# Hybrid mixer of a two-layer model: decay rows through DRAM, a side-by-side dt product, folded squares and a new order

## The chip, the cores and the metric

The kernel runs on one core of a Trainium2 chip, as one program and one launch. The metric is the device time of one execution in microseconds (us); lower is better. Three executions of the kernel before took 1096.77, 1097.22 and 1097.34 us, so the median is 1097.22 us. Durations below come from one further execution under the profiler.

The engines are named as in the profile: PE is the matrix engine (PEld its weight loads), DVE the vector engine, ACT the scalar engine, POOL is GpSimd, SP only issues transfers here. Each engine works through its own list of instructions in order. A tile is at most 128 partitions wide; "128x256" is 128 partitions by 256 elements.

## The reference

The model has two layers on 256 tokens of width 1024, all in float32. Layer 0 is FFN, hybrid mixer, FFN; layer 1 is FFN, mLSTM, FFN. A modulated RMS norm stands ahead of each. The change lies in the hybrid mixer alone:

```python
def hybrid_mixer(h, ...):
    gate_lru, x_lru, z_ssd, xbc, dt_raw = jnp.split(h @ w_in, HYB_SPLITS, axis=-1)
    x_lru = causal_conv(x_lru, lru_conv_w, lru_conv_b)
    y_lru = rg_lru(x_lru, ...) * jax.nn.gelu(gate_lru)
    xbc = jax.nn.silu(causal_conv(xbc, ssd_conv_w, ssd_conv_b))
    xs, bm, cm = ...                                   # 16 heads of 64, 2 groups, state 128
    dt = jax.nn.softplus(dt_raw + ssd_dt_bias)
    y = ssd_chunked(xs, dt, -jnp.exp(ssd_a_log), bm, cm) + ssd_d[:, None] * xs
    y = y * jax.nn.silu(z_ssd)
    y = rms_norm(y, in 2 groups of 512)
    return concatenate([y_lru, y]) @ w_out

def ssd_chunked(x, dt, a, bm, cm):                     # 2 chunks of 128 tokens
    acs = jnp.cumsum(dt * a, axis=-1)                  # per head and chunk
    decay_in = exp(acs[l] - acs[s]) for s <= l, else 0
    y_diag = einsum(cb * decay_in, x * dt)             # cb = C B^T of the chunk
    y_off = einsum(C, state of the chunk before) * exp(acs)
```

## The kernel before

Everything is held transposed: features on partitions, 256 tokens along the row. All weights come as one stream of 366 **pieces** of 512 KB (8 tiles of 128x128), sent by SP into four `wraw` buffers. ACT rounds each piece to `whi` (line 101), DVE takes the rest `wlo` (line 102); these two are the **weight split** of a piece. There are six pairs of buffers for split pieces. A weight product is three matmuls, `whi` by the high and the low part of the activation and `wlo` by the high part (lines 443, 444 and 445; `project`).

A scheduler in the framework sets the order of the instructions on each engine when the program is built, by priority and dependence. The kernel steers it in a few places. `stand(ins, s, n)` puts a PE instruction right behind the n-th weight product of stage s, `SUMS` holds such places for the sums of squares. `in_one_go` keeps a group of PE instructions together. `W.behind(i, n, ins)` orders the split n (0 is ACT's, 1 is DVE's) of piece i behind an instruction. `ADA_PLAN` spreads 144 blocks of the modulation (a 512 KB transfer and one 128x1024 DVE instruction each, line 262) over the pieces of the stages; 8 of them are in the hybrid stage, at its pieces 22 to 37.

The hybrid stage runs from about 199 to 375 us of the span. In order:

- `begin` computes B and C of the ssd; then come `xbc` 0 to 7, each a product, an ACT pass and three DVE taps (line 733) of the convolution. Behind them stand the `dtT` product (lines 818 to 820, 8 row tiles by three matmuls with the 16 columns of dt), softplus as a series in small DVE steps, the running sums `acs`, and their transpose `acst`.
- Ten steps follow with `xl` (product, ACT, three taps), `z` and the gates of the recurrence `ri`, and with the ssd's values and states in between.
- Then four **pairs** m0 = 0, 2, 4, 6 of 128 features (4 heads each). The rows of `acs` must stand on all 128 partitions. So DVE puts a high and a low part of the rows into `stk` (lines 864 and 865), and four `ab` matmuls a pair (line 974) spread them through a selector `sel` into two PSUM banks. ACT makes eight Relus of 128x128 from them (line 983), two Exps for `ce` (line 985) and one Exp over `mt` (line 986). DVE multiplies `mt` by `cb` (line 988) and `ce` by C (line 992). The 24 products `y` follow on PE (line 1008), DVE takes them out (lines 1012 and 1014), ACT squares them (lines 1018 and 1021). Behind each pair stand two `gl` products, the gate of the recurrence.
- Behind pairs 2 and 6 the squares of a group are summed over partitions (`rst_g`, line 359: two halves by two token blocks, so four matmuls of a 128x1 result, which the profile shows as eight), a chain of nine small DVE steps takes the inverse root (lines 373 and 320 to 329), and `rsb_g` (line 405) spreads it.
- `od`, the output product, reads the ssd's features 0 to 3 (`ysb`), then 4 to 7, then those of the recurrence (`ylb`), which come out of scans (line 1057) and a multiplication (line 1066).

## Time and profile before

| | |
|---|---|
| median of three executions | 1097.22 us |
| the profiled execution | 1097.25 us |
| its span (first to last instruction) | 1095.5 us |
| around the span | 1.75 us |
| PE busy | 1083.8 us, 99% |
| DVE busy | 920.5 us, 84% |
| ACT busy | 639.5 us, 58% |
| granted PE clock | 0.999 |
| moved by the DMA | 272.34 MB |

Busy times are averages over stages with different limits. Matmuls overlap: a row's mean for one matmul is longer than the step from one start to the next, so a count of matmuls is turned into time by the step. A stage's own limit is seen where an engine is busy for its whole window, and in PE's gaps with the instruction that ended each.

### The profile page before, as it was taken

To read this page: it belongs to the slowest core of one execution; us is meant where nothing else is said; L and a number is where in the kernel's file an instruction comes from. 1 tells how busy PE (TensorE), PEld (TensorE's weight loads), DVE (VectorE), ACT (ScalarE), POOL (GpSimd) and SP (SyncE) were. 2 spreads that over 40 slices of the span, in tenths; PEclk is the share of its full clock that TensorE was granted. 3 is DMA by queue.
4 is the path that set the end of the run, shared out by engine and by line. 5 is a ranking of instruction groups with operands and counts; after the bars stand their busy time and mean duration, and the time that the engine had idled before them with its cause. 6 is when DMAs were issued, how large, how long until landed. Compare 5 with 4: busy or idle time off the path is not lost.

```text
span 1095.5 us, 23272 instructions
## 1 busy us (share of the span) xinstructions
PE 1083.8 (99%) x9315; PEld 1070.4 (98%) x9315; DVE 920.5 (84%) x1654; ACT 639.5 (58%) x1053; POOL 8.8 (1%) x28
## 2 busy tenths in 40 slices
PE   9999999999999999999999999999999999999997
PEld 7999999999999999999999999999999999999997
DVE  7999999899999899989698798979768868866552
ACT  5765555678986564554454455448776655544452
POOL 0000000000000000000000000010000000000000
PEclk9999999999999999999999999999999999999999
DMA  9889999556855489999848799963432664875551
GB/s 375 344 318 391 387 352 343 178 196 195 279 167 191 139 307 370 354 351 327 281 142 323 266 356 346 338 204 119 146 102 81 208 193 137 298 239 193 193 174 39
DMA packets 75534, 272.34 MB, mean 249 GB/s; under 512 B 8593, under 2 KB 9393, under 8 KB 75426
## 3 DMA queue, kind: packets, MB, share of 16 engines
q1 hardware_dynamic: 74592, 269.38, 69.7%
q8 instruction: 73, 1.20, 0.4%
q0 software_dynamic: 400, 1.04, 0.4%
q10 hardware_dynamic: 434, 0.43, 0.1%
q14 instruction: 35, 0.29, 0.1%
HBM read 269.77 MB, written 1.05 MB: 247 GB/s over the span
## 4 chain that ended last, share of the span: by engine, by line
PE 80%; DVE 12%; DMA 4%; issue 2%; ACT 1%; ACTq 0%; DVEq 0%; SPq 0%
PE gu L445 12%; PE gu L444 12%; PE gu L443 11%; PE od L445 10%; PE od L443 10%; PE od L444 10%; DVE wlo L102 4%; DMA wraw<-in_wst_dram 3%; PE zz L445 1%; PE zz L443 1%; PE zz L444 1%; DMA wgr<-in_ml_wg_dram 1%; DVE ada L262 1%; DVE xc L733 1%; PE gu_f L509 1%
## 5 line engine op out<-in xcount | busy, mean ns | idle before, releaser
L102 DVE TENSOR_TENSOR wlo<-wraw,whi 128x1024 fp32r<-128x1024 f32 x364 | 442.9, 1221 | 83.6 <-ACT whi L101 83.0
L101 ACT CAST whi<-wraw 128x1024 fp32r<-128x1024 f32 x364 | 378.2, 1050 | 210.9 <-DMA wraw<-in_wst_dram 80.2
L444 PE MATMUL gu<-hb,whi 128*128 128x256 f32 x1296 | 358.0, 276 | 0.4 <-DVE hb L668 0.3
L443 PE MATMUL gu<-hb,whi 128*128 128x256 f32 x1296 | 358.0, 276 | 0.0
L445 PE MATMUL gu<-hb,wlo 128*128 128x256 f32 x1296 | 357.9, 276 | 0.1
L444 PEld LDWEIGHTS gu<-hb,whi 128*128 128x128 f32 x1296 | 243.3, 188 | 0.8 <-DVE hb L668 0.8
L445 PEld LDWEIGHTS gu<-hb,wlo 128*128 128x128 f32 x1296 | 243.3, 188 | 0.2 <-DVE wlo L102 0.2
L443 PEld LDWEIGHTS gu<-hb,whi 128*128 128x128 f32 x1296 | 243.2, 188 | 0.0
L443 PE MATMUL od<-ph,whi 128*128 128x256 f32 x704 | 194.3, 276 | 0.0
L444 PE MATMUL od<-ph,whi 128*128 128x256 f32 x704 | 194.3, 276 | 0.0
L445 PE MATMUL od<-ph,wlo 128*128 128x256 f32 x704 | 194.3, 276 | 0.0
L262 DVE SCALAR_TENSOR_TENSOR ada<-ada,cact 128x1024 f32<-128x1024 f32 x144 | 175.3, 1218 | 1.4 <-DMA ada<-in_adaT_dram 1.3
L444 PEld LDWEIGHTS od<-ph,whi 128*128 128x128 f32 x704 | 132.1, 188 | 0.0
L445 PEld LDWEIGHTS od<-ph,wlo 128*128 128x128 f32 x704 | 132.1, 188 | 0.0
L443 PEld LDWEIGHTS od<-ph,whi 128*128 128x128 f32 x704 | 132.1, 188 | 0.0
L426 ACT CAST ph<-fg 128x256 fp32r<-128x256 f32 x88 | 35.1, 406 | 114.9 <-DVE fg L595 114.9
L427 DVE TENSOR_TENSOR ph<-fg,ph 128x256 fp32r<-128x256 f32 x88 | 36.4, 421 | 14.2 <-ACT ph L426 14.2
L416 ACT ACTIVATE sq_o<-x 128x256 f32<-128x256 f32 x42 | 17.5, 418 | 45.6 <-DVE x L571 40.6
L571 DVE SCALAR_TENSOR_TENSOR x<-od,gate,x 128x256 f32<-128x256 f32 x48 | 23.1, 481 | 24.4 <-PE od L445 24.2
L444 PE MATMUL zz<-hb,whi 128*128 128x256 f32 x128 | 36.2, 283 | 0.0
L445 PE MATMUL zz<-hb,wlo 128*128 128x256 f32 x128 | 36.1, 282 | 0.0
L443 PE MATMUL zz<-hb,whi 128*128 128x256 f32 x128 | 35.8, 279 | 0.0
(431 smaller groups left out, 1959.1 us busy)
## 6 DMA issues: line engine op xcount, KB each, us to landing
wraw<-in_wst_dram SPq DMA_DIRECT2D x366, 512.0 KB, 4.6
ada<-in_adaT_dram SPq DMA_DIRECT2D x144, 512.0 KB, 5.6
xn<-in_x_dram SPq DMA_DIRECT2D x2, 512.0 KB, 4.0
wgr<-in_ml_wg_dram POOLq DMA_DIRECT2D x3, 256.0 KB, 5.4
out_dram<-res SPq DMA_DIRECT2D x3, 128.0 KB, 2.4
out_dram<-res ACTq DMA_DIRECT2D x1, 256.0 KB
out_dram<-res SPq DMA_DIRECT2D x1, 256.0 KB, 2.9
cols<-in_cols_dram SPq DMA_DIRECT2D x1, 190.0 KB, 9.5
```

Of the source, the lines that this page charges most:

```text
L101: raw_hi = nc.scalar.copy(hi, raw)
L102: self.last = nc.vector.tensor_tensor(out=lo, in0=raw, in1=hi.bitcast(F32), op=ALU.subtract)
L262: return nc.vector.scalar_tensor_tensor(out=raw, in0=raw, scalar=1.0, in1=cact, op0=ALU.mult, op1=ALU.mult, accum_out=mods[s][:, m:m + 1])
L416: square = nc.scalar.activation(q, x, AF.Square).ins
L426: nc.scalar.copy(hi, src)
L427: nc.vector.tensor_tensor(out=both[:, 1, :], in0=src, in1=hi.bitcast(F32), op=ALU.subtract)
L443: m = nc.tensor.matmul(dst, wh, both[:, 0, :], start=start, stop=False, skip_group_check=True)
L444: W.products += [m, nc.tensor.matmul(dst, wh, both[:, 1, :], start=False, stop=False, skip_group_check=True), nc.tensor.matmul(dst, wl, bo ...
L445: nc.tensor.matmul(dst, wl, both[:, 0, :], start=False, stop=stop, skip_group_check=True)]
L509: W.products += [nc.tensor.matmul(dst, wh, rh, start=(k == 0), stop=False), nc.tensor.matmul(dst, wh, rl, start=False, stop=False), nc.ten ...
L571: nc.vector.scalar_tensor_tensor(out=xs_t[d], in0=dst, scalar=g[:, d:d + 1], in1=xs_t[d], op0=ALU.mult, op1=ALU.add)
L733: nc.vector.scalar_tensor_tensor(out=dst[:, o:], in0=src[:, :T - o], scalar=cw(j), in1=dst[:, o:], op0=ALU.mult, op1=ALU.add)
```

## The change

Four parts, all in the hybrid stage.

**Decay rows.** `sel`, `stk` with its two DVE instructions, and the 16 `ab` matmuls are gone. ACT copies the 16 rows of `acst` to `rows`, SP sends them to a tile `kept` in DRAM (16 KB), and one transfer a pair reads four rows back to all 128 partitions of `mt` (512 KB, 4 KB to a partition). The eight Relus and Exps read `mt` from SBUF instead of PSUM, `ce` is one Exp of 128x512 instead of two of 128x256. All of that is in `decay_pair`, which for pairs 0 and 2 is called in the last steps of the loop ahead of the pairs.

**dt.** The high and low columns stand side by side in one tile `wd`, so 16 matmuls replace 24, and one more DVE add of 128x32 puts the two results together.

**Squares.** DVE adds the two halves of a group's squares (128x256), and `rst_g` has two matmuls instead of four (four records instead of eight).

**Order.** New places on PE for `y0`, `y2`, the second `rst_g` and the second `rsb_g`. Six weight splits of DVE are ordered behind steps of the chains: piece 9 behind the last tap of `xbc0`, 31 behind that of `xl7`, 37 and 40 behind the two folds, 39 behind a pair's last evacuation, 42 behind the second inverse root. The scans of `lru` stand behind the second inverse root. Two modulation blocks move from the stage's pieces 22 to 37 to its pieces 11 to 15, and the other six to 20 to 32. The first four `ysb` splits are written ahead of the second half of the pairs.

```diff
-SUMS = {"n1": (1, 11), "n2": (2, 11), "n4": (4, 14)}
+SUMS = {"n1": (1, 11), "n2": (2, 11), "n4": (4, 14), "g1": (1, 934)}
+SPREADS = {"n2": (2, 28), "g1": (1, 995)}
...
-    (0, (17, 43), range(16, 40)), (0, (43, 65), range(48, 64)), (1, (22, 37), range(40, 48)),
+    (0, (17, 43), range(16, 40)), (0, (43, 65), range(48, 64)), (1, (11, 15), range(40, 42)),
+    (1, (20, 32), range(42, 48)),
...
+    dramp = ctx.enter_context(tc.tile_pool(name="dramp", bufs=1, space=bass.MemoryType.DRAM))
...
-            if nm == "n2" and b == 0:
-                stand(m, 2, 28)
+            if b == 0 and nm in SPREADS:
+                stand(m, *SPREADS[nm])
...
-    dt_parts = [cst.tile([P, 8 * 16 + 112], F32R, name=n) for n in ("wdh", "wdl")]
+    dt_parts = cst.tile([P, 480], F32R, name="wd")
...
-        for w in dt_parts:
-            nc.gpsimd.memset(w[:, 128:240].bitcast(F32), 0.0)
-        wdh, wdl = (w[:, 0:128].rearrange("p (k h) -> p k h", k=8) for w in dt_parts)
+        nc.gpsimd.memset(dt_parts[:, 256:352].bitcast(F32), 0.0)
+        wdh, wdl = (dt_parts[:, 0:256].rearrange("p (k i h) -> p k i h", k=8, i=2)[:, :, i] for i in range(2))
...
             for i, b in enumerate(two):
                 xbc(xs[:, i, :], b[:, 0:T], i)
+                if i == 0:
+                    W.behind(starts[1] + 9, 1, taps[-1])
...
         b = ax_bank("dtT")
         for k in range(ND):
-            wdh, wdl = (w[:, 16 * k:16 * k + P] for w in dt_parts)
-            nc.tensor.matmul(b[:, 0:T], wdh, h[k][:, 0, :], start=(k == 0), stop=False)
-            nc.tensor.matmul(b[:, 0:T], wdh, h[k][:, 1, :], start=False, stop=False)
-            nc.tensor.matmul(b[:, 0:T], wdl, h[k][:, 0, :], start=False, stop=(k == ND - 1))
+            for i in range(2):
+                nc.tensor.matmul(b[:, 0:T], dt_parts[:, 32 * k:32 * k + P], h[k][:, i, :], start=(k == i == 0),
+                                 stop=(k == ND - 1 and i == 1))
...
-        nc.vector.tensor_tensor(out=dt, in0=b[:, 0:T].rearrange("p (c h) -> p c h", c=2)[:, :, 0:16],
-                                in1=hv[:, 0].unsqueeze(1).to_broadcast([P, 2, 16]), op=ALU.add)
+        both = b[:, 0:T].rearrange("p (c h) -> p c h", c=2)
+        nc.vector.tensor_tensor(out=dt, in0=both[:, :, 0:16], in1=hv[:, 0].unsqueeze(1).to_broadcast([P, 2, 16]),
+                                op=ALU.add)
+        nc.vector.tensor_tensor(out=dt, in0=both[:, :, 16:32], in1=dt, op=ALU.add)
...
-        stk = sp.tile([P, T], F32R, name="stk")
-        nc.gpsimd.memset(stk.bitcast(F32), 0.0)
+        rows = sp.tile([P, T], F32, name="rows")
+        kept = dramp.tile([16, T], F32, name="kept")
...
-            nc.vector.tensor_copy(stk[0:16, :], b[0:16, 0:T])
-            nc.vector.tensor_tensor(out=stk[32:48, :], in0=b[0:16, 0:T], in1=stk[0:16, :].bitcast(F32),
-                                    op=ALU.subtract)
-
+            nc.scalar.copy(rows[0:16, :], b[0:16, 0:T])
+            nc.sync.dma_start(kept, rows[0:16, :])
+
+        def decay_tile(m0):
+            mt = wk.tile([P, 2, 2, 2, P], F32, tag="mt", name=f"mt{m0}", bufs=2)
+            nc.sync.dma_start(mt.rearrange("p n i c t -> p (n i c t)"),
+                                kept.rearrange("(q h) t -> q (h t)", q=4)[m0 // 2:m0 // 2 + 1].to_broadcast([P, 4 * T]))
+            decays[m0] = mt
+
+        decays = {}
...
-        sel = sp.tile([P, 16], F32R, name="sel")
+        sp.tile([P, 16], F32R, name="pad3")
...
-            nc.vector.tensor_tensor(out=sel, in0=ident[:, 0:16], in1=ident[:, 32:48], op=ALU.add)
...
+        def decay_pair(m0):
+            g = m0 // 4
+            mt = decays.pop(m0)
+            ce = wk.tile([P, 2, 2, P], F32, tag="ce", name=f"ce{m0}", bufs=2)
+            expo = nc.scalar.activation(ce.rearrange("p n i t -> p (n i) t"),
+                                        mt.rearrange("p n i c t -> p (n i) c t")[:, :, 1, :], AF.Exp)
+            for n in range(2):
+                for i in range(2):
+                    for c in range(2):
+                        hd = 2 * (m0 + n) + i
+                        nc.scalar.activation(mt[:, n, i, c, :], mt[:, n, i, c, :], AF.Relu,
+                                             bias=acs[:, c, hd:hd + 1], scale=-1.0)
+            nc.scalar.activation(mt, mt, AF.Exp, scale=-1.0)
...
+            return mt, ce, needed, expo
...
                 conv(xl[:, c, :], b[:, 0:T], lambda j: col("lru_cw", 8 * j + c), col("lru_cb", c), c, 8)
+                if c == 7:
+                    W.behind(starts[1] + 31, 1, taps[-1])
...
                 xw = ssd_values(c // 2 - 1)
             if c in (4, 6):
                 ssd_state(c // 2 - 2, xw)
-
-        roots = []
+            if c in (5, 7):
+                decay_tile(c - 5)
+            if c in (7, 9):
+                pairs[c - 7] = decay_pair(c - 7)
...
-            ab = [ax_bank(f"ab{m}") for m in pair]
-            for m, b in zip(pair, ab):
-                for i in range(2):
-                    hd = 2 * m + i
-                    nc.tensor.matmul(b[:, i * T:(i + 1) * T], sel[:, hd:hd + 1].to_broadcast([P, P]), stk,
-                                     start=True, stop=True)
-            mt = wk.tile([P, 2, 2, 2, P], F32, tag="mt", name=f"mt{m0}", bufs=2)
-            ce = wk.tile([P, 2, 2, P], F32, tag="ce", name=f"ce{m0}", bufs=2)
...
-                expo = nc.scalar.activation(ce[:, n], b.rearrange("p (i t) -> p i t", i=2)[:, :, P:T], AF.Exp)
-            nc.scalar.activation(mt, mt, AF.Exp, scale=-1.0)
...
+            mt, ce, needed, expo = pairs.pop(m0) if m0 in pairs else decay_pair(m0)
...
             in_one_go(products, needed)
+            if m0 < 4:
+                stand(products[0], 1, (732, 795)[m0 // 2])
...
-            nc.vector.scalar_tensor_tensor(out=xs[:, m0:m0 + 2, :], in0=xs[:, m0:m0 + 2, :], scalar=0.5,
-                                           in1=sz[:, m0:m0 + 2, :], op0=ALU.mult, op1=ALU.mult)
+            evacuated = nc.vector.scalar_tensor_tensor(out=xs[:, m0:m0 + 2, :], in0=xs[:, m0:m0 + 2, :], scalar=0.5,
+                                                       in1=sz[:, m0:m0 + 2, :], op0=ALU.mult, op1=ALU.mult)
...
                 nc.vector.tensor_tensor(out=gacc, in0=gacc, in1=q, op=ALU.add)
+                folded = nc.vector.tensor_tensor(out=gacc[:, 0, :], in0=gacc[:, 0, :], in1=gacc[:, 1, :], op=ALU.add)
+            if m0 < 4:
+                decay_tile(m0 + 4)
...
             if m0 % 4 == 2:
-                roots.append(rs_tokens([gacc[:, 0, :], gacc[:, 1, :]], 512, f"g{g}", "q"))
+                roots.append(rs_tokens([gacc[:, 0, :]], 512, f"g{g}", "q"))
                 if g == 0:
                     group_norm(0)
...
-        ys = [sp.tile([P, 2, T], F32R, tag=f"ssd{m % 4}{m // 4}", name=f"ysb{m}") for m in range(8)]
-        for m in range(4):
-            split(xs[:, m, :], ys[m])
...
+                if g == 0:
+                    W.behind(starts[1] + 37, 1, folded)
+                else:
+                    W.behind(starts[1] + 39, 1, evacuated)
+                    W.behind(starts[1] + 40, 1, folded)
+                    W.behind(starts[1] + 42, 1, rsqrt_ends[-1])
+                ys += [sp.tile([P, 2, T], F32R, tag=f"ssd{m}{g}", name=f"ysb{4 * g + m}") for m in range(4)]
+                if g == 0:
+                    for m in range(4):
+                        split(xs[:, m, :], ys[m])
+        second_root = rsqrt_ends[-1]
...
-                nc.vector.tensor_tensor_scan(out=xl[:, c, :], data0=av[:, c, :], data1=nq[:, c, :], initial=0.0,
-                                             op0=ALU.mult, op1=ALU.add)
+                with tc.issue_after(second_root.ins):
+                    nc.vector.tensor_tensor_scan(out=xl[:, c, :], data0=av[:, c, :], data1=nq[:, c, :], initial=0.0,
+                                                 op0=ALU.mult, op1=ALU.add)
```

What the scheduler makes of it, at three places. First PE at the first pair. Before, the last `ri` product, the `ab` spreads and the first `gl`:

```order
L444 MATMUL ri_3968<-xlb_3828,whi_3768 128x256
L445 MATMUL ri_3968<-xlb_3828,wlo_3769 128x256
L974 MATMUL ab_3984<-stk,sel 128x256 x2
L974 MATMUL ab_3985<-stk,sel 128x256 x2
L443 MATMUL gl_4023<-hb,whi_3814 128x256
L444 MATMUL gl_4023<-hb,whi_3814 128x256
L445 MATMUL gl_4023<-hb,wlo_3815 128x256
L443 MATMUL gl_4023<-hb,whi_3814 128x256
```

and, 60 rows on, the first `y`, in the midst of the third `gl`:

```order
L445 MATMUL gl_4130<-hb,wlo_3899 128x256
L443 MATMUL gl_4130<-hb,whi_3898 128x256
L1008 MATMUL y_4005<-mt_3990,ssd_2618 64x128 x2
L1008 MATMUL y_4005<-mt_3990,ssd_2620 64x128 x2
L1008 MATMUL y_4005<-ce_3991,ssd_2622 64x128 x2
L1008 MATMUL y_4005<-mt_3990,ssd_2618 64x128 x2
L1008 MATMUL y_4005<-mt_3990,ssd_2620 64x128 x2
L1008 MATMUL y_4005<-ce_3991,ssd_2622 64x128 x2
L444 MATMUL gl_4130<-hb,whi_3898 128x256
```

With the change `y` of the first pair (its `mt` and `ce` are made in the loop ahead) stands in the midst of the first `gl`, and no `ab` is left:

```order
L447 MATMUL gl_4032<-hb,whi_3814 128x256
L448 MATMUL gl_4032<-hb,wlo_3815 128x256
L1026 MATMUL y_4012<-mt_3692,ssd_2618 64x128 x2
L1026 MATMUL y_4012<-mt_3692,ssd_2620 64x128 x2
L1026 MATMUL y_4012<-ce_3885,ssd_2622 64x128 x2
L1026 MATMUL y_4012<-mt_3692,ssd_2618 64x128 x2
L1026 MATMUL y_4012<-mt_3692,ssd_2620 64x128 x2
L1026 MATMUL y_4012<-ce_3885,ssd_2622 64x128 x2
L446 MATMUL gl_4032<-hb,whi_3814 128x256
L447 MATMUL gl_4032<-hb,whi_3814 128x256
```

The first `y` products now come 12 matmuls behind the last `ri` instead of 62.

Second SP, whose queue holds every weight piece (`wraw`) and modulation block (`ada`) in the order of use. Before, some pieces ahead of the first pair:

```order
L95 DMA wraw_3733<-in_wst_dram 128x1024
L95 DMA wraw_3766<-in_wst_dram 128x1024
L95 DMA wraw_3812<-in_wst_dram 128x1024
L260 DMA ada_3856<-in_adaT_dram 128x1024
L95 DMA wraw_3850<-in_wst_dram 128x1024
L260 DMA ada_3945<-in_adaT_dram 128x1024
L95 DMA wraw_3896<-in_wst_dram 128x1024
L95 DMA wraw_3939<-in_wst_dram 128x1024
L260 DMA ada_4062<-in_adaT_dram 128x1024
L95 DMA wraw_4024<-in_wst_dram 128x1024
L95 DMA wraw_4056<-in_wst_dram 128x1024
```

At the same place of the change the rows go out (`kept<-rows`) and come back (`mt`) within this queue, the first two in one go:

```order
L872 DMA kept<-rows 16x256
L97 DMA wraw_3695<-in_wst_dram 128x1024
L97 DMA wraw_3733<-in_wst_dram 128x1024
L263 DMA ada_3818<-in_adaT_dram 128x1024
L97 DMA wraw_3769<-in_wst_dram 128x1024
L97 DMA wraw_3812<-in_wst_dram 128x1024
L263 DMA ada_3917<-in_adaT_dram 128x1024
L876 DMA mt_3692<-kept 128x1024
L876 DMA mt_3883<-kept 128x1024
L97 DMA wraw_3853<-in_wst_dram 128x1024
L97 DMA wraw_3911<-in_wst_dram 128x1024
L263 DMA ada_4039<-in_adaT_dram 128x1024
```

What stands behind an `mt` transfer in this list is issued only once its buffer is free; the third and the fourth follow nine and thirteen rows behind the second.

Third DVE at the second group's inverse root. Before, each small step has a weight split, a 128x1024 product or a scan behind it:

```order
L324 SCALAR_TENSOR_TENSOR rsw_g_4438<-rsw_g_4438,rsv_g_4436 128x2
L1057 SCALAR_TENSOR_TENSOR lru_x<-lru_aq 128x256
L325 SCALAR_TENSOR_TENSOR rsw_g_4438<-rsw_g_4438 128x2
L1057 SCALAR_TENSOR_TENSOR lru_x<-lru_aq 128x256
L326 SCALAR_TENSOR_TENSOR rsy_g_4439<-rsw_g_4438,rsy_g_4439 128x2
L1057 SCALAR_TENSOR_TENSOR lru_x<-lru_aq 128x256
L327 TENSOR_TENSOR rsw_g_4438<-rsy_g_4439 128x2
L1057 SCALAR_TENSOR_TENSOR lru_x<-lru_aq 128x256
L328 SCALAR_TENSOR_TENSOR rsw_g_4438<-rsw_g_4438,rsv_g_4436 128x2
L1057 SCALAR_TENSOR_TENSOR lru_x<-lru_aq 128x256
L329 SCALAR_TENSOR_TENSOR rsy_g_4439<-rsw_g_4438,rsy_g_4439 128x2
L102 TENSOR_TENSOR wlo_4557<-wraw_4554,whi_4556 128x1024
```

With the change the steps follow each other, and the scans and the next splits come behind:

```order
L326 TENSOR_TENSOR rsw_g_4416<-rsy_g_4417 128x2
L327 SCALAR_TENSOR_TENSOR rsw_g_4416<-rsw_g_4416,rsv_g_4414 128x2
L328 SCALAR_TENSOR_TENSOR rsw_g_4416<-rsw_g_4416 128x2
L329 SCALAR_TENSOR_TENSOR rsy_g_4417<-rsw_g_4416,rsy_g_4417 128x2
L330 TENSOR_TENSOR rsw_g_4416<-rsy_g_4417 128x2
L331 SCALAR_TENSOR_TENSOR rsw_g_4416<-rsw_g_4416,rsv_g_4414 128x2
L332 SCALAR_TENSOR_TENSOR rsy_g_4417<-rsw_g_4416,rsy_g_4417 128x2
L1087 SCALAR_TENSOR_TENSOR lru_x<-lru_aq 128x256
L104 TENSOR_TENSOR wlo_4441<-wraw_4438,whi_4440 128x1024
L1005 SCALAR_TENSOR_TENSOR ssd_x<-ssd_x,cols,rsb_g_4456 128x256 x4
```

Five scans have moved from between the steps to behind the chain.

29 lines of the change are left out of this document (13 added, 16 removed).

## The prediction

> **What bounds the kernel now.** I read the profile by stages first. In the view of windows the columns are the window, its length, busy time (count) of PE, PEld, DVE, ACT and POOL, then the clock and the DMA's share.
>
> ```profile
> 235.00:287.00 52.00, 51.23 (x440) 50.07 (x439) 51.68 (x113) 43.00 (x82) 0.00 (x0) 1.00 0.62 207
> 287.00:335.00 48.00, 46.27 (x435) 44.39 (x434) 46.97 (x89) 43.36 (x94) 0.00 (x0) 1.00 0.57 188
> ...
> 372.00:550.00 178.00, 178.00 (x1568) 178.00 (x1567) 156.76 (x245) 93.47 (x136) 1.07 (x2) 1.00 0.87 315
> ...
> 285.00:295.00 10.00, 9.93 (x86) 9.72 (x86) 10.00 (x18) 9.97 (x25) 0.00 (x0) 1.00 0.88 291
> ```
>
> From 372 to 550 us PE never stops: 178.00 us for 1568 matmuls, 0.1135 us from start to start. That is its pace, and there any matmul less is time less. In the hybrid stage (first two rows) PE has gaps and DVE is busy instead: 51.68 of 52 and 46.97 of 48 us. So two engines are at their limit at once, and each part of the change must be asked whether PE or DVE would have set the time there. From 285 to 295 us ACT is full as well, 9.97 of 10.
>
> Second, the waits of PE between 190 and 375 us (total, times, longest), which is the whole list, and the larger places in PE's timeline (start, length, instruction):
>
> ```profile
> PE y L1008 <- DVE mt L988: 0.8, 1, 0.8
> PE z L443 <- DVE lru_x L733: 0.8, 1, 0.8
> PE rsb_g L405 <- DVE rsy_g L329: 0.7, 1, 0.7
> PE xbc L443 <- DVE ssd_x L733: 0.3, 1, 0.3
> ...
> 282.85 0.28 PE L445 MATMUL ri<-xlb,wlo 128*128 128x256 f32 x1
> 283.90 0.39 PE L443 MATMUL z<-hb,whi 128*128 128x256 f32 x1 [0.77 <-DVE lru_x L733]
> ...
> 293.41 0.97 PE L974 MATMUL ab<-stk,sel 128*128 128x256 f32 x4
> 294.22 0.28 PE L443 MATMUL gl<-hb,whi 128*128 128x256 f32 x1
> ...
> 295.28 0.28 PE L443 MATMUL gl<-hb,whi 128*128 128x256 f32 x1
> 296.41 0.44 PE L1008 MATMUL y<-mt,ssd 128*64 128x128 f32 x4 [0.85 <-DVE mt L988]
> ...
> 330.61 0.28 PE L445 MATMUL od<-ysb,wlo 128*128 128x256 f32 x1
> 331.61 0.46 PE L405 MATMUL rsb_g<-ident,rsy_g 128*128 128x128 f32 x2 [0.72 <-DVE rsy_g L329]
> ```
>
> Every stall is ended by a chain step on DVE, none by a weight split (line 102). What it costs is the step between the two starts less the pace of 0.1135: 0.94 (`z`), 1.02 (`y`) and 0.89 (`rsb_g`), and 0.3 for `xbc` by the list, in sum 3.15. The second `ab` block takes 294.22 − 293.41 = 0.81 where another takes 0.47 (below), so 0.34 more. Together 3.5 us of stalls.
>
> **The matmuls taken away.** The chain of waits (start, length, what) has the small blocks, and the step of a weight split on DVE:
>
> ```profile
> 291.40 1.14 DVE wlo L102
> ...
> 308.22 0.87 PE rst_g L359 x8
> 311.19 0.47 PE ab L974 x4
> ...
> 323.37 1.04 PE rst_g L359 x8
> ```
>
> Four `ab` blocks at 0.47 are 1.9 us. `dtT` loses 8 of its 24 matmuls: 8 × 0.1135 = 0.9. Each `rst_g` halves: 2 × 0.87 / 2 = 0.9. In sum 3.7 us of PE's own time; with all stalls 3.7 + 3.5 = 7.2, the ceiling. No PE instruction is added.
>
> **What DVE does more or less.** Rows of the groups (busy, mean ns):
>
> ```profile
> L864 DVE CAST stk<-acst 16x256 fp32r<-16x256 f32 x1 | 0.4, 402 | 0.0
> L865 DVE TENSOR_TENSOR stk<-acst,stk 16x256 fp32r<-16x256 f32 x1 | 0.4, 415 | 0.0
> L427 DVE TENSOR_TENSOR ysb<-ssd_x,ysb 128x256 fp32r<-128x256 f32 x8 | 2.9, 418 | 0.0
> 235.73 0.18 DVE L832 TENSOR_TENSOR dt<-dt,hv 128x32 f32<-128x32 f32 x1
> ```
>
> The two `stk` steps go (0.8), two folds of 128x256 come (0.8 by the `ysb` row of the same shape), and a second add of 128x32 (0.2). Nothing is gained: DVE has the same work in the stage, and it was busy 98.65 of the 100 us of the first two windows. So a PE that runs ahead meets DVE. How far can it? The last thing PE needs of DVE here is the last split of `ylb`, and its use, the seventh tile of the recurrence's features in the output product:
>
> ```profile
> 347.06 0.69 DVE L433 TENSOR_TENSOR ylb<-lru_x,ylb 128x512 fp32r<-128x512 f32 x1
> 352.21 0.28 PE L443 MATMUL od<-ylb,whi 128*128 128x256 f32 x1
> ```
>
> It is done at 347.75 and used at 352.2 (the last group of `od`, over six features, starts at 350.85, twelve matmuls ahead): 4.5 us of room. To this comes what DVE idled in the two windows, 1.35 us, so far as earlier releases fill it. PE can thus gain at most some 5.9 us before DVE's end binds, and 4.5 without any of DVE's idle time. That is below the ceiling of 7.2. What the new order does is to say which DVE work is late: six weight splits go behind chain steps. As no wait of PE is on a split now, the splits have a lead, and one that is later by one or two DVE instructions costs nothing; without the lead each would cost up to its 1.14 us.
>
> **The single waits, each from both sides.** Where DVE is with a step is an estimate: along its new list I add up the step of each kind in the trace (1.14 for a 128x1024 split, about a third of a 128x1024 for 256 wide), from the start of the stage, where nothing has changed. The `y0` products move up by 50 matmuls, from 296.4 to about 286.5 with the earlier gains counted. Their `ce` leaves DVE at 286.7 to 287.9 by that sum, so this stall is between 0.2 and 1.4 instead of 1.02; I take 0.8. The `z` stall: its tap now stands ahead of a split of 1.14, a gain of up to 0.94, but PE comes there 2 us earlier; 0 to 2, I take 1. `xbc`: also a tap ahead of a split of 1.14, from 0.3 to 0. The first `rst_g` now waits for a fold besides the squares' sum, and PE reaches it earlier: between 0 and 2, I take 1.2. The second inverse root took from the end of `rst_g` at 324.4 to `rsb_g` at 331.6, with splits, products and scans between its nine steps; nine steps of 0.18 (the 128x32 row) are 1.6 us, so that stall goes (0 to 0.9, I take 0). The extra 0.34 goes with `ab`. The stalls are then 3.0 instead of 3.5: little is won there, PE only arrives earlier. 3.7 + 0.5 = 4.2 us, and DVE's room says 4.5; I take 4.4. **Forecast: 1097.25 − 4.4 = 1092.85, rounded to 1092.8 us**; the profiled execution lies 0.03 above the median, so no correction is made.
>
> **Transfers and ACT.** Rows of the DMA issues (count, KB, us to landing) and of ACT:
>
> ```profile
> wraw<-in_wst_dram SPq DMA_DIRECT2D x366, 512.0 KB, 4.6
> out_dram<-res SPq DMA_DIRECT2D x3, 128.0 KB, 2.4
> L983 ACT ACTIVATE mt<-ab,acs 128x128 f32<-128x128 f32 x32 | 9.9, 417 | 0.0
> L985 ACT ACTIVATE ce<-ab 128x256 f32<-128x256 f32 x8 | 3.6, 453 | 0.0
> L929 ACT ACTIVATE a<-lru_aq 128x256 f32<-128x256 f32 x8 | 3.3, 414 | 0.1
> L1027 ACT COPY ssd_z<-gl 128x256 f32<-128x256 f32 x8 | 2.6, 377 | 0.0
> ```
>
> The trace has no such broadcast. Bounds: as a weight piece of the same 512 KB, 4.6 us, or longer, as all 128 partitions read one 4 KB row of DRAM; I take 4.6. Out and back is 2.4 + 4.6 = 7 us. By the place in SP's list `mt0` is issued at about 267, and its Relus come on ACT at about 278, so this is hidden, and for `mt2` more so. The third must wait until the first `y` has read its buffer, at about 288, lands at about 293 to 294 and is read by ACT at an estimated 295.5: 1.5 to 2 us to spare. The fourth, by the same count, has about 2. The weight pieces behind them on SP's queue wait for DVE's splits anyway, so I put that at nothing.
>
> On ACT the Relus now read SBUF. The rows nearest are `a<-lru_aq` (from SBUF, 414 ns) and `ssd_z<-gl` (from PSUM, 377 ns), both 128x256: 37 ns more, 0.3 us a pair; two `ce` of 128x256 become one of 128x512, which saves about as much. So ACT stays where it is, and I count nothing; with ACT full from 285 to 295 us, 0.3 us a pair would cost at most 0.6 for the two pairs made by then, if nothing were saved. [...]
>
> **The rivals.**
>
> *PE takes it all.* The order puts every chain ahead of time, DVE's idle 1.35 us fill up, and PE's stalls all go: 7.2 us, or 1090.0. For it: every stall named has an order put against it. Against it: DVE's work is the same, and 7.2 is above its 5.9. Own range 1089 to 1091.3, chance 0.2.
>
> *DVE decides alone, the stalls grow by what PE saves.* PE arrives 3.7 us earlier and waits at `y0` (1.4), `z` (2.0), the fold (2.0) and the next pair (0.8), 6.2 instead of 3.5; 3.7 − 2.7 = 1.0, or 1096.2. For it: the full DVE rows. Against it: 4.5 us of room at `ylb`. Own range 1095 to 1097.3; chance 0.2.
>
> *The broadcast is slow.* If the read-back takes t instead of 4.6, `mt4` and `mt6` are late by t − 6.6 each beyond their 2 us, ACT stands at the Relu, behind it stand the copies of `gl` that free PE's banks, and on SP the weight pieces. From t = 8.8 us on, twice that eats the gain; at 10 us it is 2 × 3.4 = 6.8, and the time 1097.25 − 4.4 + 6.8 = 1099.7, slower. For it: 128 readers of one row, and the DMA's share of 0.88 just there. Against it: its bytes are those of a weight piece. Own range 1099.4 to 1105, chance 0.1.
>
> **How the numbers follow.** The forecast's case has 0.5, own range 1091.3 to 1095. A difference of 0.2% or 2.2 us is about what can be told from none in this kernel. Faster is the forecast's case (0.5), PE's (0.2) and a fifth of DVE's (0.04): 0.74. Same is the rest of DVE's, 0.16; slower 0.10. The range of 1089.0 to 1097.3 holds the first three cases and leaves out the slow broadcast.
>
> **What would show it.** Right: no PE gap above 0.3 us at the second `rsb_g` and at `xbc1`; DVE still busy over 98% from 235 to 335; the last `ylb` split within 2 us of its use; ACT not waiting on `mt<-kept`; the stage's output product ending about 4.4 us earlier, and all later stages of the same length. Wrong: a landing of `mt<-kept` above 6.6 us, or a `y` waiting on ACT; the gain would then be less. Where the `ylb` split still has 4 us of room, PE has taken all or other stalls have grown, and the size of the gain tells which.

## The result: slower, by 7.3 us

The changed kernel takes 1104.57 us (median of four executions, 1103.47 to 1107.18), the kernel before beside it 1097.28 (four, 1096.77 to 1097.9). The ratio is 1.007, with a 95% interval of 1.005 to 1.0089. The forecast was 1092.8, in a range up to 1097.3, so the direction was wrong and not only the size. The profiled execution took 1107.18 us; its span is 1105.5, 10.0 longer than before's, and it is the longest of the four, so its stalls stand for somewhat more than the median.

Where the time went, by the starts of the same instructions in PE's timeline:

| first instruction of | before, us | after, us | difference |
|---|---|---|---|
| `bc`, the stage's start | 193.71 | 194.98 | +1.3 |
| `xl` | 233.02 | 233.14 | +0.1 |
| `gl` | 287.92 | 291.67 | +3.8 |
| `y` of the first pair | 296.41 | 293.15 | −3.3 |
| `od` from `ysb` | 320.83 | 323.01 | +2.2 |
| `od` from `ylb` | 345.41 | 347.49 | +2.1 |
| `gu` of the next FFN | 380.17 | 388.64 | +8.5 |

So the time was lost at two places: between `xl` and `gl`, and far more behind the stage's end. The 1.3 us at `bc` lie ahead of the stage; e1 and e2 below, which are alike up to there, start it at 194.09 and 194.16, so most of this seems to be this execution's own. What was foreseen did happen: the side-by-side dt and the first tap win 1.2 us by `xl`, and `y` comes 3.3 us earlier in spite of the loss ahead of it. PE's waits from 190 to 385 us (total, times, longest):

```profile
PE st L924 <- DVE xw L916: 3.5, 2, 2.1
PE rst_n L362 <- ACT sq_o L419: 2.8, 1, 2.8
PE od L447 <- DVE ylb L436: 0.5, 1, 0.5
PE rst_g L362 <- DVE gacc L1043: 0.5, 1, 0.5
```

The four stalls of the prediction (`z`, `y`, `rsb_g`, `xbc`) are gone, and two others stand there: `st`, a state of the ssd, and `rst_n`, the sums of squares ahead of the next FFN, which lies behind the hybrid stage. What is late at `st` is shown by DVE's waits from 200 to 372 us (the longest one after, and the same wait before), and by the timeline of ACT, DVE and PE after:

```profile
DVE xlb L430 <- ACT xlb L429: 4.9, 4, 1.4
...
DVE xlb L427 <- ACT xlb L426: 0.3, 1, 0.3
...
257.76 1.05 ACT L103 CAST whi<-wraw 128x1024 fp32r<-128x1024 f32 x1 [0.89 <-DMA wraw<-in_wst_dram]
259.18 0.39 ACT L429 CAST xlb<-lru_x 128x256 fp32r<-128x256 f32 x1
...
259.60 0.42 DVE L430 TENSOR_TENSOR xlb<-lru_x,xlb 128x256 fp32r<-128x256 f32 x1 [1.43 <-ACT xlb L429]
261.48 0.68 DVE L916 TENSOR_TENSOR xw<-ssd,dec 128x512 f32<-128x512 f32 x1
...
262.31 1.10 PE L924 MATMUL st<-xw,bnat 128*128 128x512 f32 x2 [2.14 <-DVE xw L916]
```

A weight cast that waits for its transfer (0.89 us, then 1.05 of its own) now stands ahead of the cast of `xlb` in ACT's list, and that one starts at 259.18; DVE waits for that (1.43 us), `xw` is late, and PE with it. DVE waited 4.9 us for the casts of `xlb` in four places, 0.3 in one before. The two windows in which the prediction found DVE full, and the stretch behind `rst_n`, in the view of windows (columns as there):

```profile
235.00:287.00 52.00, 48.48 (x410) 46.88 (x409) 48.02 (x105) 41.00 (x83) 0.00 (x0) 1.00 0.68 224
287.00:335.00 48.00, 46.92 (x438) 44.59 (x436) 44.98 (x90) 43.86 (x86) 0.00 (x0) 1.00 0.55 187
372.00:374.00 2.00, 0.00 (x0) 0.00 (x0) 1.73 (x5) 0.97 (x4) 0.00 (x0) 0.86 0.79 293
374.00:376.00 2.00, 1.70 (x8) 1.70 (x9) 0.48 (x1) 0.64 (x2) 0.00 (x0) 0.50 0.33 133
376.00:378.00 2.00, 2.00 (x10) 2.00 (x11) 1.52 (x10) 0.00 (x0) 0.00 (x0) 0.50 0.00 0
378.00:380.00 2.00, 2.00 (x11) 2.00 (x11) 1.07 (x1) 0.00 (x0) 0.00 (x0) 0.50 0.00 0
380.00:382.00 2.00, 2.00 (x18) 2.00 (x17) 0.88 (x2) 0.77 (x2) 0.00 (x0) 0.93 0.72 260
```

DVE is busy 93.0 of 100 us instead of 98.65: it was not full, it was kept waiting. And after PE's standstill at `rst_n` the granted clock is 0.50 for 6.8 us (the shares below 1.00, summed over the five rows): PE does 10 or 11 matmuls in 2 us where it does 18 or 19.

Why `rst_n` is late: before, it had nothing to spare. The last `x`, its square and the sums, before (timeline, and the tile's own view with min/median/max ns and first and last start):

```profile
367.47 0.48 DVE L571 SCALAR_TENSOR_TENSOR x<-od,gate,x 128x256 f32<-128x256 f32 x1
368.05 0.42 ACT L416 ACTIVATE sq_o<-x 128x256 f32<-128x256 f32 x1 [1.03 <-DVE x L571]
...
L359 PE MATMUL rst_n<-ones,sq_o x4: 250/250/271, 368.5 to 368.9; 128*128 128x1 f32 x4
```

The same `x` in the timeline of the changed kernel:

```profile
373.26 0.47 DVE L574 SCALAR_TENSOR_TENSOR x<-od,gate,x 128x256 f32<-128x256 f32 x1
```

The square ends at 368.47 and the sums start at 368.5. So the last thing that PE needs of DVE is not the last `ylb` split but this `x`, with no room at all. In the changed kernel it begins 5.8 us later, though `od` from `ylb` was 2.1 late: the weight splits, and with them DVE's whole list, run late. ACT's wait for the transfers of pieces from 320 to 372 us, after and before:

```profile
ACT whi L103 <- DMA wraw<-in_wst_dram: 10.0, 7, 4.3
...
ACT whi L101 <- DMA wraw<-in_wst_dram: 2.0, 3, 1.0
```

A late split frees its `wraw` buffer late, so the next piece is sent late (what SP waits for longest from 200 to 380 us is DVE's `wlo`, 128.3 us in 49 times after and 131.0 in 46 before), ACT waits for it, and the next split is later still. How far ahead the splits are is seen by the lead: from the end of DVE's split of a piece to the first product that reads it, by both timelines (pieces counted from the start of the stage; the last four columns are kernels of the experiments below):

| piece | before | after | blocks back (e1) | early blocks, no late order (e3) | blocks back, no late order (n1) | before + late scans and split 42 (o1) |
|---|---|---|---|---|---|---|
| 39 | 18.0 | 0.5 | 0.5 | 12.3 | 11.7 | 18.0 |
| 43 | 11.9 | 0.0 | 0.0 | 16.1 | 13.3 | 2.7 |
| 45 | 5.1 | 0.8 | 0.8 | 11.7 | 7.6 | 2.4 |
| 49 | 6.7 | 2.2 | 2.3 | 9.5 | 8.0 | 3.5 |

### The profile page after: what moved, and what is told of

It is laid out like the page before. It is cut to its first block, busy times and chain, and to the rows that moved or that the text cites. A ratio compares the mean times of both kernels' runs of the same rounds, so it can differ in the third digit from the quotient of the medians.

```text
span 1105.5 us, 23195 instructions
## 1 busy us (share of the span) xinstructions
PE 1086.1 (98%) x9283; PEld 1071.0 (97%) x9283; DVE 920.6 (83%) x1654; ACT 640.4 (58%) x1050; POOL 8.4 (1%) x26
## 4 chain that ended last, share of the span: by engine, by line
PE 73%; DVE 13%; DMA 7%; ACT 5%; issue 2%; ACTq 0%; DVEq 0%; SPq 0%
PE gu L447 11%; PE gu L448 11%; PE gu L446 11%; PE od L447 9%; PE od L446 9%; PE od L448 9%; DMA wraw<-in_wst_dram 5%; DVE wlo L104 4%; ACT whi L103 1%; PE zz L448 1%; PE zz L446 1%; PE zz L447 1%; DMA wgr<-in_ml_wg_dram 1%; DVE hb L479 1%; DVE xc L738 1%
```

## The experiments

The theories: the transfers hold up SP's queue (T1); the late splits and scans cost the stream its lead (T2); the early modulation blocks delay casts and splits (T3); the end of the stage, with the last `x` behind splits and the clock after it, makes the loss (T4); DVE's sum of work sets the time in any order (T5). Ratios are to the kernel before, run beside, with 95% intervals.

### One part undone

**The modulation blocks back at pieces 22 to 37 (e1).**

```diff
-    ... (1, (11, 15), range(40, 42)),
-    (1, (20, 32), range(42, 48)),
+    ... (1, (22, 37), range(40, 48)),
```

> The changed kernel with one part undone: the eight modulation blocks of the hybrid stage are back at its pieces 22 to 37. Three theories. T1, transfers: the row transfers kept<-rows and mt<-kept hold up the weight pieces behind them on SP's queue, and so eat the lead of the splits; under it this run stays within 1103 to 1107 us. T2, late splits: the splits ordered behind the chains use up the lead until PE waits, and the gap ahead of the next norm drops the clock; under it also 1103 to 1107. T3, order on ACT: a weight cast that waits for its piece now stands ahead of the casts of xlb, so DVE and then PE (the two st products, 3.5 us) wait; if the early modulation blocks are what moved it, this run has no st wait above 0.5 us and takes 1099 to 1101 us.

1100.91 us, 1.0034 [1.0022, 1.0046]: half of the loss is gone. `st` does not wait any more. `od` from `ysb` starts at 317.64, 3.2 us ahead of before, and from `ylb` at 343.04, 2.4 ahead. PE's longest waits are now

```profile
PE rst_n L361 <- ACT sq_o L418: 2.5, 1, 2.5
PE od L445 <- ACT ysb L428: 1.3, 1, 1.3
```

and behind `rst_n` the clock is 0.50 for 6.8 us; `gu` is 3.8 late. So the rows, dt and fold do win what PE no longer has to do, and the end of the stage takes back more than twice as much.

**The transfers of the rows on GpSimd's queue (e2).**

```diff
-            nc.sync.dma_start(kept, rows[0:16, :])
+            nc.gpsimd.dma_start(kept, rows[0:16, :])
-            nc.sync.dma_start(mt.rearrange(...
+            nc.gpsimd.dma_start(mt.rearrange(...
```

> The changed kernel with kept<-rows and the four mt<-kept issued on GpSimd's queue instead of SP's, so that no weight piece waits behind them. T1 (transfers): SP's waits of 4.7 us at kept and 5.4 us at mt vanish, the lead of the splits at the stage's pieces 39 to 44 grows from about 0.5 us to 4 us or more, the gap ahead of the next norm (2.8 us) goes, and the time is 1095 to 1099 us. T2 and T3: the waits on SP vanish too, but the splits wait for DVE anyway, and the time stays at 1102 to 1106 us.

1108.13 us, 1.0098 [1.0083, 1.0113], no better and above both ranges; `st` waits 3.3 us and `rst_n` 2.7 as in the changed kernel, and the lead is 0.5 and 0.1 us at pieces 39 and 43 as there. T1 falls: taking the rows off SP's queue gives the stream no lead back. Why this kernel is slower still was not looked into; `z` and `rst_g` wait 2.1 us each in its trace.

**Without the late order (e3).**

```diff
-                if g == 0:
-                    W.behind(starts[1] + 37, 1, folded)
-                else:
-                    W.behind(starts[1] + 39, 1, evacuated)
-                    W.behind(starts[1] + 40, 1, folded)
-                    W.behind(starts[1] + 42, 1, rsqrt_ends[-1])
...
-                with tc.issue_after(second_root.ins):
```

> The changed kernel without the four weight splits ordered behind the folds, the evacuation and the second inverse root, and without the scans ordered behind that root. T2 (late splits): lead at pieces 39 to 44 back above 4 us, no wait of PE ahead of the next norm, granted clock 1.00 throughout, 1098 to 1100 us. T1 and T3: DVE is behind already at piece 32 (8 us later than before the change), so the lead stays below 3 us and the time is 1102 to 1106 us.

1105.73 us, 1.0078 [1.0063, 1.0093]. The lead is back (table) and `rst_n` does not wait, but now the chains stand behind the splits:

```profile
PE rsb_g L408 <- DVE rsy_g L332: 2.8, 1, 2.8
PE st L924 <- DVE xw L916: 2.1, 1, 2.1
PE od L446 <- ACT ysb L429: 1.6, 2, 1.4
```

With the early blocks in place the late order only moves the loss; T2 alone does not explain it. The time lies in the range of T1 and T3, but their sign, a lead below 3 us, did not come.

### One part alone, on the kernel before

**dt and the fold (b1).** The edit is the change's own for `wd`, the second add and `folded`, without any order.

> The kernel before with only the side-by-side dt product (16 for 24 matmuls) and the folded squares (two for four matmuls a group). By the sum of PE's work this is 0.9 + 0.9 = 1.8 us: 1095.4 us, if nothing else moves. T3 (order on ACT): the shorter dt product already moves a weight cast ahead of an xlb cast, so an st wait of 1 to 2.5 us shows and the time is 1096.5 to 1099 us. T1 and T2 say nothing against 1095.4.

1098.54 us, 1.0013 [1.0003, 1.0022]. PE's 24 → 16 matmuls and the halved sums are worth 1.8 us by PE's pace, and the next DVE steps take them all and some 1.4 us more: `rsb_g` waits 1.4 instead of 0.7, `od` 0.9 for `ysb`.

**The early blocks (f3).**

```diff
-    ... (1, (22, 37), range(40, 48)),
+    ... (1, (11, 15), range(40, 42)),
+    (1, (20, 32), range(42, 48)),
```

> The kernel before with only the early modulation blocks (two at the stage's pieces 11 to 15, six at 20 to 32). T3: the blocks alone push a weight cast ahead of the xlb casts on ACT, two st waits of 1 to 2.5 us each show, and the time is 1099 to 1101 us. Rival: the blocks do harm only together with the shorter dt product, and the time is 1096.5 to 1098 us.

1104.92 us, 1.0066 [1.0047, 1.0085]: this part alone costs as much as the whole change, and more than T3 had expected. T3 holds so far that the blocks do it without the rest. The waits at `st` and `rst_n` are at the places of the changed kernel's, the one at `z` is new:

```profile
PE z L444 <- ACT thi L923: 1.8, 1, 1.8
PE st L913 <- DVE xw L905: 1.6, 2, 1.1
PE rst_n L360 <- ACT sq_o L417: 0.9, 1, 0.9
```

Whether it is a block's step on DVE, its transfer ahead of a piece, or the new order of ACT's casts that does it was not taken apart.

**The rows (d1).** The change without the blocks' move, dt, fold, late order, the two early splits (9 and 31), and the places of `g1`.

> The kernel before with only the decay rows through DRAM (no ab products, early pairs 0 and 2, the places of y0 and y2), everything else as before. By PE's work 1.9 us and the extra 0.34 us of ab go, and the wait ahead of y0 of 1.0 us may shrink: 1094 to 1095.5 us if DVE and the transfers bear it. T1 (transfers on SP's queue hold up the weight pieces): the lead of the splits falls below 3 us somewhere and the time is 1097 us or more.

1101.59 us, 1.004 [1.0026, 1.0055]. `y` starts at 289.0, 7.4 earlier, and `od` from `ysb` at 320.42, 0.4 earlier; then `rsb_g` waits 1.9 and `od` 1.8 for `ysb`, the clock is 0.50 for 3.4 us, and `od` from `ylb` is 4.2 late. The lead stays above 7 us at pieces 37 to 53, so a lost lead is not what costs here.

**dt and the tap (b2).**

```diff
+                if i == 0:
+                    W.behind(starts[1] + 9, 1, taps[-1])
```

with the dt part of b1.

> The kernel before with only the side-by-side dt product and the split of the stage's piece 9 behind the last tap of xbc0. By PE's sum 0.9 us of matmuls and up to 0.4 us of the xbc wait go: 1095.9 to 1096.5 us. T5 (PE's savings in this stage are given back at the next DVE step): 1096.8 to 1098 us, with the waits at z, y and rsb_g longer by what was saved.

1097.64 us, 1.0001 [0.9991, 1.001]: no difference. `xl` is 0.9 earlier (232.15 against 233.02), `od` from `ysb` 0.2, and by `ylb` nothing is left.

### The end of the stage

**Two splits behind the last x (f1), and idle transposes ahead of the sums (f2), both on e1.**

```diff
+            if s == 1 and n == ND - 1:
+                W.behind(starts[1] + 56, 1, out_end)
```

> The run with the modulation blocks put back (1100.9 us), and in it the weight splits of the stage's pieces 56 and 57 on DVE ordered behind the last evacuation of the output product, so that these 1.14 us steps no longer stand between the evacuations. T4, the tail: the splits that were put behind the chains are made up between the evacuations of the output product, 2.3 us a round on DVE against 2.04 us on PE, so the last sum of squares is 2.5 us late, PE stands still for 2.7 us, and the granted clock falls to 0.5 for some 6.5 us, 3.3 us more. Under T4 the gap falls to below 1 us, the clock stays at 1.00, and the time is 1094 to 1096.5 us. Rival: the evacuations are late for another reason, and the time stays at 1100 to 1102 us.

1101.1 us, 1.0028 [1.0017, 1.0039]; `rst_n` waits 3.1. The first `x` was late already, behind three splits. Behind it DVE does without the two splits, but stands four times 0.55 us for ACT's squares and once 1.4 us for a weight cast, so the last `x` begins at 368.43 as in e1 (368.41), and the edit saves nothing.

```diff
+            if nm == "n2":
+                products = [nc.tensor.transpose(pt[:, P:2 * P], ident, ident) for _ in range(24)]
```

> The run with the modulation blocks put back (1100.9 us), and in it 24 idle transposes of 128x128 on PE just ahead of the sum that it waits 2.5 us for, so that PE does not stand still. It separates the wait from the clock. If the drop of the clock to 0.5 comes from PE standing still, the clock stays at 1.00 and 3.0 to 3.5 us come back, though the wait itself stays: 1097 to 1098.5 us. If the clock falls for another reason: 1100 to 1102 us, with the clock at 0.5 again.

1099.7 us, 1.0023 [1.0013, 1.0032]. The order of the rest shifted with it: the standstill came at `od`, 3.0 us from 330.62 on, with the clock at 0.50 behind it, and none at the sums. So this run could not tell the cost of the clock, and the next two were made.

**A late x on the kernel before, without and with idle transposes (c1, c2).** Eight steps of DVE that multiply the last `x` by one, and the products of the next FFN held behind the sums; c2 adds 26 transposes, and all other instructions are alike.

```diff
+            if s == 1 and n == ND - 1:
+                for _ in range(8):
+                    nc.vector.scalar_tensor_tensor(out=xs_t[d], in0=xs_t[d], scalar=1.0, in1=xs_t[d],
+                                                   op0=ALU.mult, op1=ALU.max)
...
+    for n in range(11, 60):
+        tc.add_manual_dep(W.products[3 * PIECE * starts[2] + n].ins, pins[0].ins.name, NOSYNC, ...)
```

> The kernel before, with eight more DVE steps of 128x256 on the last tile of x ahead of the sums of squares behind the hybrid stage (they multiply by one), and PE's products held behind those sums, so that PE must stand there. Eight steps at about 0.40 us are 3.2 us. If a standstill costs only its own length: 1097.3 + 3.2 = 1100.5 us, the granted clock 1.00 in the windows behind it. If PE's clock falls after a standstill of this length, as the traces since the change show at this place (0.50 for 4 to 6.5 us, worth 2 to 3.3 us): 1102.5 to 1103.8 us.

> The same as the one with the late x, and 26 transposes of the identity whose results nobody reads stand on PE right ahead of the sums, where PE would stand idle: 26 steps of about 0.11 us, 2.9 us, so that about 0.3 us of standstill is left. The DVE list and all other PE instructions are the same. If a standstill costs only its length, both take the same 1100.5 us. If the clock is what costs more: 1100.5 us here, the clock 1.00 behind the place, and 2 to 3.3 us less than the kernel without the transposes.

c1 1103.44 us (1103.05 to 1105.28), 1.0055 [1.0043, 1.0068]; c2 1101.51 (1101.0 to 1102.15), 1.0036 [1.0023, 1.0049]. Windows of c1, then of c2:

```profile
370.00:372.00 2.00, 0.00 (x0) 0.00 (x0) 1.58 (x4) 0.22 (x1) 0.00 (x0) 0.73 0.27 109
372.00:374.00 2.00, 1.75 (x9) 1.75 (x9) 0.00 (x0) 0.59 (x2) 0.00 (x0) 0.50 0.00 0
374.00:376.00 2.00, 2.00 (x10) 2.00 (x11) 1.61 (x10) 0.00 (x0) 0.00 (x0) 0.50 0.00 0
376.00:378.00 2.00, 2.00 (x13) 2.00 (x12) 1.28 (x2) 0.00 (x0) 0.00 (x0) 0.57 0.04 8
```

```profile
372.00:374.00 2.00, 1.64 (x14) 1.64 (x15) 0.51 (x3) 0.71 (x2) 0.00 (x0) 1.00 0.03 8
374.00:376.00 2.00, 2.00 (x19) 1.87 (x17) 1.79 (x9) 0.00 (x0) 0.00 (x0) 1.00 0.00 0
376.00:378.00 2.00, 2.00 (x19) 2.00 (x19) 1.75 (x4) 1.20 (x3) 0.00 (x0) 1.00 0.19 47
```

The sums start at the same time in both (372.25 and 372.36), yet `gu` at 386.36 and 384.21. So the low clock alone costs 1.9 us by the medians, 2.15 in these two executions, beside some 3.9 for the standstill itself (1101.51 − 1097.65). T4 holds for the clock.

### Less DVE work in the stage

**Four modulation blocks out of the stage, on before (h1) and on e1 (h2), and all eight on e1 (h3), into the FFN ahead.**

```diff
-    ... (0, (43, 65), range(48, 64)), (1, (22, 37), range(40, 48)),
+    ... (0, (43, 65), list(range(40, 44)) + list(range(48, 64))), (1, (22, 37), range(44, 48)),
```

> The kernel before, with four of the eight modulation blocks of the hybrid stage (1.22 us of DVE each, 4.9 us) moved into the first FFN stage, where DVE idles 10.4 of 162 us. T5: DVE's work sets the hybrid stage, and PE's stalls there (3.5 us) shrink with it: 1094 to 1096.3 us. Rival: the first stage's transfers are full (DMA share 0.94) and four more blocks of 512 KB cost there what the hybrid stage gains, or the order on DVE, not its sum, makes the stalls: 1096.8 to 1099 us.

> The changed kernel with the modulation blocks put back to pieces 22 to 37 (1100.9 us), and four of these eight moved on into the first FFN stage. T5: 4.9 us less of DVE work gives the late splits their lead back (above 3 us at the stage's pieces 39 to 47 instead of 0 to 1.6), the wait ahead of the next norm falls below 1 us and the clock does not drop: 1093.5 to 1097 us. Rival (the tail's wait has its own cause in the evacuations' order): 1099 to 1101 us.

> As the run before it, with all eight blocks (9.8 us of DVE) moved into the first FFN stage. T5: no wait of PE above 1 us left in the hybrid stage, 1091 to 1095 us, if the first stage bears the 4 MB more; if its transfers or DVE do not, its end is 1 to 4 us later and the time 1094 to 1098 us. Rival as before: 1098 to 1101 us.

h1 1103.79 us, 1.0055 [1.0037, 1.0072]; h2 1100.49, 1.0026 [1.0016, 1.0036]; h3 1106.02, 1.0074 [1.0055, 1.0093]. Four blocks less are some 4.6 us less of DVE in the stage (4 × 1.14), and the kernel before gets slower by them: it stands 2.2 us at an `xbc` behind the new order and has the clock at 0.50 twice, for 3.4 us each. h2 is like e1 within its spread, and h1 and h3 are above all their ranges. PE's longest waits in h1, then in h2:

```profile
PE xbc L443 <- DVE ssd_x L733: 2.2, 1, 2.2
...
PE rst_n L361 <- ACT sq_o L418: 2.4, 1, 2.4
```

This is no clean test of T5, as the blocks went to the pieces just ahead of the stage. `xl` comes 5.1 us later in h1 than before, and 2.4 and 7.7 later in h2 and h3 than in e1; from `xl` to `od` from `ylb` the stage is then shorter, by 1.0, 2.2 and 1.9 us. That speaks for less DVE work helping inside the stage, but its head loses as much or more. As the claim that the sum decides in any order T5 falls all the same, by f3 and by the next pair: the same work in another order is slower by 7.6 and by 2.9 us.

### The second root's order alone

**Scans and the split of piece 42 behind the second root, on before (o1) and on b2 (o2).**

```diff
+                else:
+                    W.behind(starts[1] + 42, 1, rsqrt_ends[-1])
+        second_root = rsqrt_ends[-1]
...
+                with tc.issue_after(second_root.ins):
                     nc.vector.tensor_tensor_scan(...
```

> The kernel before, with two pieces of the order alone: the scans stand behind the second inverse root, and the split of piece 42 too. Theory (the chain kept together helps by itself as long as no split loses its lead): the stall of 0.89 us at the second spread goes, 1096.4 us. Rival (DVE's sum sets the stage): what the chain wins the scans give back at the recurrence's splits, 1097.3 us. Slower than 1097.9 would say that the scans or the split are late by themselves.

> The same two pieces of order on top of the kernel before with the side-by-side dt product and the split of piece 9 behind the first tap: if the gains add and none is given back, 1097.3 - 1.15 - 0.89 = 1095.3 us. If DVE gives back what PE wins (as with the dt product alone, 1097.6), 1097.0 to 1097.6 us.

o1 1100.53 us, 1.0023 [1.0012, 1.0035]; o2 1101.27, 1.0034 [1.0022, 1.0046]: two places of the order, slower by 2.9 us. The stall at `rsb_g` falls from 0.7 to 0.2, and `od` from `ylb` starts 0.85 earlier. The timeline of DVE at the chain's first steps and the first `x`, before and then o1:

```profile
325.64 0.16 DVE L320 TENSOR_SCALAR rsy_g<-rsv_g 128x2 int32<-128x2 int32 x1
325.70 1.22 DVE L1055 SCALAR_TENSOR_TENSOR lru_aq<-lru_x,lru_aq 128x1024 f32<-128x1024 f32 x1
...
353.21 0.48 DVE L571 SCALAR_TENSOR_TENSOR x<-od,gate,x 128x256 f32<-128x256 f32 x1
```

```profile
324.13 0.16 DVE L373 TENSOR_SCALAR rsv_g<-rst_g 128x2 f32<-128x2 f32 x1 [0.93 <-PE rst_g L359]
324.32 0.17 DVE L320 TENSOR_SCALAR rsy_g<-rsv_g 128x2 int32<-128x2 int32 x1
324.52 0.16 DVE L323 TENSOR_TENSOR rsw_g<-rsy_g 128x2 f32<-128x2 f32 x1
...
355.35 0.48 DVE L571 SCALAR_TENSOR_TENSOR x<-od,gate,x 128x256 f32<-128x256 f32 x1
```

Before, between long instructions, a step of the chain adds 0.06 us to DVE's list (325.64 to 325.70) and overlaps with its neighbours: the product behind it starts while the step's own 0.16 us still run. In o1, behind the step whose result it reads, it starts 0.19 to 0.20 after that one's start, so 0.03 to 0.04 after its end. Nine steps are 1.65 us instead of some 0.55, and DVE stands 0.93 more ahead of them, where a split filled the time: 2.0 us in all. The first `x` is 2.1 us later, `rst_n` waits 2.1, and the clock is 0.50 for 3.4 us. Packing the chain shortens the path that PE waits on here and takes DVE's time from every split behind it. The two places were not undone one by one on this kernel.

**e1 without the late order (n1), and o2 with piece 42's split left free (o3).**

> The change with the modulation blocks back at their old places and without the late splits of pieces 37, 39, 40, 42 and the late scans: the decay rows, the dt product, the fold and the two early splits are left. If the lost lead of the weight stream is what costs (with the blocks back alone: 1100.9 us, a standstill of 2.5 us at the sums and the clock at 0.50), the lead comes back to over 10 us at pieces 39 to 45, the sums' standstill goes, and the time is 1096 to 1098 us. If the chain steps behind the splits cost as much as the splits behind the chain (as with the early blocks, where leaving out the late order changed nothing): 1099.5 to 1102 us, with waits of 1.5 us and more at the second spread or at the output product's first operands.

> The kernel before with the side-by-side dt product, the split of piece 9 behind the first tap, and the scans behind the second root, but the split of piece 42 left free. The scheduler now puts three weight splits and two products of 128x1024 between the second root's steps. So the weight stream keeps its lead (at piece 43 over 10 us as before), no standstill at the sums, and instead the second spread waits: 5 instructions at 1.14 us where two splits and four scans of 0.60 stood, so 1 to 3 us more stall there: 1097.5 to 1100.5 us, all of it at the spread. If the stand at the sums comes back although the lead is kept, the lost lead isn't its cause.

n1 1098.49 us, 1.0011 [1.0002, 1.002]; o3 1099.8, 1.0022 [1.0012, 1.0031]. In both the lead is kept and `rst_n` does not wait. In n1 `od` from `ysb` starts at 317.58, 3.25 us ahead of before, and then

```profile
PE od L445 <- ACT ysb L428: 1.7, 1, 1.7
PE od L446 <- DVE ysb L429: 0.9, 2, 0.6
...
PE rsb_g L407 <- DVE rsy_g L331: 0.7, 1, 0.7
```

with 3.4 us at half clock: the gain is gone by `ylb` (346.81, 1.4 late). o3 waits 1.4 at the same `od`, not at the spread as expected: the stall moved one step down the chain. The lead and the standstill at the sums go together: with 7 us and more at piece 45 (d1, e3, n1, o3) there is none, with 0.8 to 2.4 us (the changed kernel, e1, e2, f1, h3, o1, o2) it is 1.7 to 3.1 us. That the lead is the cause is not shown. h2 has 6.0 us at piece 43 and 3.7 at 45, and `rst_n` still waits 2.4; h1 has 5.2 at 45 as the kernel before has 5.1, and waits 1.2 where that one waits nothing. What is late in all of them is DVE's list as a whole. The last `x` begins 0.4 us behind the start of the last `od` product in the kernel before, d1, e3, n1 and o3, and 2.9 in h2, 3.1 in e1 and 3.3 in the changed kernel. Keeping the lead sends the wait back to the chain.

The loss of 7.3 us can be undone in two steps: putting the blocks back takes off 3.7 us (e1), leaving out the late order as well another 2.4 (n1). What is left is 1.1 us above the kernel before, and the 4.4 us that were forecast do not appear. No kernel here beats the one before. b2 equals it, and of those with the decay rows n1, the change without its blocks and its late order, comes nearest.

## Why the prediction was wrong, point by point

**PE's own time was about right.** 3.7 us of matmuls taken away were forecast; e1 and n1 reach the output product 3.2 us earlier, and b2's `xl` comes 1.15 earlier, counted from `bc`, where 0.9 for dt and 0.3 for the tap were forecast.

**Transfers and ACT were right for the changed kernel, not for all that share the rows.** Rows of the changed kernel, and ACT's wait in e1:

```profile
mt<-kept SPq DMA_DIRECT2D x4, 512.0 KB, 4.9
...
L955 ACT ACTIVATE mt<-mt,acs 128x128 f32<-128x128 f32 x32 | 10.4, 405 | 0.0
L949 ACT ACTIVATE ce<-mt 128x512 f32<-128x512 f32 x4 | 2.5, 635 | 0.0
L871 ACT COPY rows<-acst 16x256 f32<-16x256 f32 x1 | 0.3, 344 | 0.0
...
ACT ce L948 <- DMA mt<-kept: 1.4, 1, 1.4
```

4.9 us against the 4.6 taken, and ACT does not wait on `mt` in the changed kernel. In the other kernels with the rows the transfer takes 5.6 to 7.0 us, and in six of them (e1, f1, f2, d1, h3, n1) ACT does wait for it, 0.4 to 2.8 us in all. The longest, 7.0, is 0.4 beyond the 6.6 above which the rival of the slow broadcast begins to cost; what those waits cost was not tested. The Relu from SBUF takes 405 ns here and 400 to 440 in the other kernels with the rows, against 417 from PSUM before, where 37 more were taken; no kernel here shows as much.

**"The last thing PE needs of DVE here is the last split of ylb" was the first false step.** Behind it come eight `x` and the sums, and the last `x` had 0.0 us to spare before the change. The room of 4.5 us was read at the wrong instruction; the real room of the stage was nothing.

**"One that is later by one or two DVE instructions costs nothing" was the second.** The splits were not later by one or two. A chain step waits for PE or ACT, DVE waits with it (in the changed kernel 4.9 us for ACT's casts of `xlb`, 0.7 for `rsb_g`, 0.5 for ACT's `mt`), and the split behind waits for both; the lead at pieces 39 and 43 went from 18 and 12 us to 0.5 and 0, and as buffer, transfer, cast and split follow each other in a ring, only half of it was won back within the stage (6.2 us at piece 53, 11.4 before).

**"Nothing is gained: DVE has the same work" counted work, not time.** The nine steps of the second root were priced at 0.18 each for their latency alone. What packing them costs DVE, 1.1 us and the 0.93 ahead of them, was left out (o1).

**The modulation blocks had no term at all.** The front part names their move, and the sum passes over it. It is the largest single piece that was tried: +7.6 us alone (f3), 3.7 within the change.

**The clock had no term either.** It was 0.999 throughout before, so nothing in that profile spoke of it; its price, 1.9 us for a spell of 6.8 us (c1 against c2), lies on top of a standstill.

**The rivals.** *DVE decides alone* had the direction: what PE saves, it waits for again. It is what b2 shows, at 1097.6; b1, at 1098.5, gives back more than it saved. But it bounded the loss by the saving, and a new order can lose more than it saved. No rival let a part of the order itself be slower.

By the list of what would show it: the stalls at `rsb_g` and `xbc` are gone, as said, and the last split of `ylb` did become tight (PE waits 0.5 us for it). DVE over 98% busy failed (93), and that was the sign that the sum's basis had gone. The output product's end was not 4.4 us earlier but 2.9 later (its last product starts at 369.93 instead of 367.06), and the next stage was slowed by the clock.
